# Two empty steps in the preparation of a delta-rule chunk, and shorter steps, in a hybrid flow-matching layer

## The chip, the cores and the metric

The kernel runs on one core of one Trainium2 chip. The metric is the device time of one execution in microseconds (us). The version before took 2160.81 us in the median of 3 runs (2158.47 to 2161.46). The engines are named as in the profile: PE is TensorE's matrix multiply and PEld its weight load, DVE is VectorE, ACT is ScalarE, POOL is GpSimd, and SP is SyncE, which only issues transfers here.

## The reference

One layer is applied to 2048 sample tokens and to 128 prompt tokens. Tokens are normalized and modulated, one wide projection gives the columns of three branches, each branch is gated and projected back, the three results are merged by sigmoid gates, and an output projection and a last norm follow.

```python
def mixer(xn, w_in, conv_w, a_log, dt_bias, o_norm_g, sgu_norm_g, w_spatial, b_spatial, w_branch, w_out, s0_f, s0_b, grid):
    proj = jnp.einsum('btd,de->bte', xn, w_in)
    qkv, beta, dec, z_a, u_b, v_b, z_b, x_c, z_c, gates = jnp.split(proj, points, axis=-1)
    qkv = short_conv(qkv, conv_w).astype(jnp.float32)
...
    o, s_f, s_b = delta_bidir(q, k, v, g, beta, s0_f, s0_b)      # branch A
    o_a = rmsnorm(o, o_norm_g) * silu(z_a)
    o_b = chunk_sgu(u_b, v_b, sgu_norm_g, w_spatial, b_spatial) * silu(z_b)
    o_c = fourier_mix(x_c, grid) * silu(z_c)
    pb = jnp.einsum('btnw,nwd->btnd', jnp.stack([o_a, o_b, o_c], axis=2), w_branch)
    merged = jnp.einsum('btnd,btnd->btd', jax.nn.sigmoid(gates), pb)
    return jnp.einsum('btd,de->bte', merged, w_out), s_f, s_b
```

Branch A is a gated delta rule in both directions over chunks of tokens. For each chunk it needs the products of the keys with each other and of the queries with the keys, and the inverse of a unit triangular matrix per head; then a scan over the chunks carries a 128x128 state per head.

## The kernel before

**Stages.** Every product of float32 matrices is made of three float16 products (high by high, high by low, low by high), so almost every value is split into a high half (ACT) and a low half (DVE). TensorE runs through the foreground in this order: the modulated tokens and branch A's gate, the q, k and v projections with their convolutions, branch B's v (the spatial gating, "sg" and "vs" in the profile), B's u and gate in four groups ("vrow"), branch C's Fourier mixing in four groups ("xc", "Y", "X", "yT"), the merge of branches B, C and A, and the output projection.

**The background.** Branch A's delta rule is a generator, `delta()`. It is advanced by `pace`: each foreground unit reports what it costs TensorE with `pace.tick`, and `Pace.steps` (L331 on) takes one step of the generator for each `quota` us so reported. The quota is `QUOTA` (1.6) during the preparation and `SCAN` (1.39) from the scan on. A step is what lies between two `yield`s. What each step issues goes into the instruction streams of all engines beside the foreground's, and a scheduler then orders each engine's stream; the engines execute their streams strictly in that order.

**Preparation of one chunk.** There are 17 chunks of 128 tokens, in five groups of 1, 4, 4, 4 and 4; below they are counted from first to seventeenth in this order. `prep` (L694) has seven steps for a chunk. Step 1 turns the keys (`turned(1)`: four transposes on TensorE, L702, of the tile "kq") and norms them into `tok` (DVE, L719). Step 2 turns the values ("kq" too) and the queries ("qr", L702), and splits the queries (L728, L729). Step 3 turns the normed keys back (L735) into the high and low halves of `T` (ACT L736, DVE L737). Step 4 makes the twelve products of T with itself on TensorE and the first of two scaled matrices on DVE (L751), its diagonal blocks (ACT L753) and its halves (L755, L756); step 5 makes the second. Step 6 stores the diagonal blocks (POOL, L760), makes the products of queries and T, and the first of two scaled results (DVE L766, ACT L768, DVE L769); step 7 makes the second. All these products go to three PSUM banks in rotation (`ps_d`). So the values are turned into the bank that the products of T had, which DVE's L751 must have read, and the queries into the bank that the products of queries and T had, which L766 must have read.

**The base inverses.** For each group, `base_inverse` (L780) inverts the 32x32 diagonal blocks on DVE: it loads them (SP, L789), lets eight steps pass, copies a half (L792), runs 31 pairs of dependent small operations (L799, L800), and splits the result (ACT L806, DVE L807, four times). `delta()` advances the base of one group by one step after each step of `prep` of the next group; its eight waiting steps add no `yield` there, its 19 others add one each. The base of the last group runs beside the scan.

**The scan.** After the last chunk, `scan()` loads the stored pieces and carries the state forward and backward. `finish_delta` takes whatever is left of it at the start of the last column block of the merge of branch C.

Of the kernel before, what the change touches and what calls it, by code (L numbers as in the profile page):

```python
# [28 lines left out]
WB = 512  # L29
EPS = 1e-6  # L30
C_QKV, C_BD, C_ZA, C_U, C_V, C_ZB, C_XC, C_ZC, C_G = 0, 1536, 1552, 2064, 2576, 3088, 3600, 4112, 4624
QUOTA = 1.6
SCAN = 1.39
MT = 0.015
XB = 4
# [76 lines left out]
def hybrid_flow_kernel(ctx: ExitStack, tc: tile.TileContext, x_prompt, x_sample, state_delta, c, c_ctx, ln_g, w_ada,  # L112
# [6 lines left out]
    def nm(s):  # L119
        uid[0] += 1  # L120
        return f"{s}_{uid[0]}"
# [4 lines left out]
    def sb(pl, shape, tag, dt=F32, bufs=None):  # L126
        kw = {} if bufs is None else {"bufs": bufs}
        return pl.tile(list(shape), dt, tag=tag, name=nm(tag), **kw)
# [11 lines left out]
    def bank(pl, shape, tag="b"):  # L140
        if pl is ps_d:
            rot[0] += 1
            pl = ps_d[rot[0] % 3]
        return pl.tile(list(shape), F32, tag=tag, name=nm(tag))
# [18 lines left out]
    def mm3(out, l, r):  # L163

        mm(out, l[0], r[0], True, False)
        mm(out, l[0], r[1], False, False)
        mm(out, l[1], r[0], False, True)
# [511 lines left out]
    def rows(part, t):  # L679
        x = sb(d2, [P, H, P], "kq" if part else "qr", bufs=3 if part else 2)  # L680
        SY.dma_start(x, qkvD[part * 4:part * 4 + 4, :, chunk_off(t):chunk_off(t) + P].rearrange("h p t -> p h t"))
        return x
# [3 lines left out]
    def late(dst, src):  # L686

        if owed:
            SY.dma_start(*owed.pop())
        if dst is not None:  # L690
            owed.append((dst, src))

    def prep(g, ci, t, nxt, held):
# [18 lines left out]
        def more(key, make):  # L712
            if nxt is not None:
                held[key] = make()
# [14 lines left out]
        V.scalar_tensor_tensor(Q16[:, 1, :], qr, qs, Q16[:, 0, :], ALU.mult, ALU.subtract)  # L729
        yield 1  # L730
        G.dma_start(kvD[t], tok)
        T = sb(d2, [P, 2, WB], "T", F16)
        ps = bank(ps_d, [P, WB])
        for h in range(H):
            PE.transpose(ps[:, hs(h)], tok[:, 0, hs(h)], ident)  # L735
        A.activation(T[:, 0, :], ps, AF.Copy, scale=FS)  # L736
        V.scalar_tensor_tensor(T[:, 1, :], ps, FS, T[:, 0, :], ALU.mult, ALU.subtract)  # L737
        more(2, lambda: rows(2, nxt))
        late(qTD[t], Q16)
        yield 1  # L740
        late(kTD[t], T)
        dc = cur["dc"]
        ps = bank(ps_d, [P, WB])
        pair = lambda t_, h: (t_[:, 0, hs(h)], t_[:, 1, hs(h)])
        for h in range(H):
            mm3(ps[:, hs(h)], pair(T, h), pair(T, h))
        nd = sb(d2, [P, 2, H, 32], "nd", bufs=2)
# [14 lines left out]
        for h in range(H):  # L762
            mm3(ps[:, hs(h)], pair(T, h), pair(Q16, h))
        for d in range(2):
# [324 lines left out]
    def delta():  # L1089
        nonlocal dq  # L1090
        seq = [(g, ci, t) for g, ts in enumerate(GROUPS) for ci, t in enumerate(ts)]
        held = {1: rows(1, 16), 2: rows(2, 16), 0: rows(0, 16), "dc": decay_rows(16)}
        yield from bounds()
        base = iter(())
        for i_, (g, ci, t) in enumerate(seq):
            if ci == 0 and g:
                for r_ in base:
                    if r_:
                        yield 1
                base = base_inverse(g - 1)  # L1100
            for n_, _ in enumerate(prep(g, ci, t, seq[i_ + 1][2] if i_ < 16 else None, held)):
                yield 1
                if next(base, 0):
                    yield 1
        late(None, None)
        for r_ in base:
            if r_:
                yield 1
        base = base_inverse(4)
        dl.close()  # L1110
        dq = pool(dl, "dqb", 1, side="right")
        V.tensor_scalar(rq, rq, bnds[:, 2:3], None, ALU.mult)
        V.tensor_scalar(beta, beta, FS, None, ALU.mult)
        for d in range(2):
            V.tensor_tensor(eg[:, d], eg[:, d], rq, ALU.mult)
        pace.quota, pace.fine = SCAN, True
        for i_, _ in enumerate(scan()):
            yield 1
            if i_ % 3 == 0:
                next(base, 0)  # L1120
        dl.close()
        dps.close()

    pace.start(delta(), QUOTA)

# [735 lines left out]
```

## Time and profile before

| | before |
|---|---|
| median of 3 runs, us | 2160.81 (2158.47 to 2161.46) |
| the profiled execution, us | 2162.01 |
| its span, first to last instruction, us | 2160.1 |
| mean granted TensorE clock | 0.994 |
| PE busy, us (share of the span) | 2098.5 (97%) |
| DVE busy, us (share) | 1403.5 (65%) |
| ACT busy, us (share) | 1057.6 (49%) |
| instructions | 43209 |

The profile comes from one execution, which ran 1.2 us above the median of the runs; 1.9 us of its time lie outside its span. In a row of a timeline stand the start, the duration, the engine, the line with its operation and, in brackets, how long the engine had been idle before it and what ended that. In a row of the waits stand the waiting instruction, what it waited for, the sum in us, how many times, and the longest. In a row of a table of stretches stand the stretch in us, the busy time of each engine with its count of instructions, the granted clock, the share of the DMA engines and GB/s. In a row of the groups stand line, engine, operation and shapes, the count, the busy time and the mean of one in ns, and the idle time before them.

### The profile page before, as it was taken

Reading aid. Unit: us, or ns where it says so; the run is one execution under the profiler, and the core shown is the slowest. Engines: PE = TensorE matmul, PEld = TensorE weight load, DVE = VectorE, ACT = ScalarE, POOL = GpSimd, SP = SyncE. Lnnn points to the kernel's source line nnn. Section 1 sums busy time; section 2 is a strip of 40 time slices with the busy share of each in tenths; the row PEclk is TensorE's granted clock in tenths of the full one; section 3 lists DMA queues with packets and bytes.
Section 4 is the critical chain, followed back from the end, with each engine's and each line's share of the span. In section 5 each row is a group of like instructions: output and inputs, shape, how many; then the busy total and the mean of one; then the engine's idle time right before and its main releaser. Section 6 shows DMA issues by size and latency. Waiting matters only on the chain.

```text
span 2160.1 us, 43209 instructions
## 1 busy us (share of the span) xinstructions
PE 2098.5 (97%) x16275; PEld 1208.3 (56%) x16275; DVE 1403.5 (65%) x3241; ACT 1057.6 (49%) x2463; POOL 735.8 (34%) x872
## 2 busy tenths in 40 slices
PE   7999999999999999999999999999999999999898
PEld 3555444455555577788656556555564444444344
DVE  5745855469888697776665546765564546754685
ACT  3644644445556565554654445655553435323452
POOL 1430533232333334233322223354542221224662
PEclk9999999999999999999999999999999999999999
DMA  8434733266776765444565555767665547544554
GB/s 278 145 94 138 265 103 111 92 191 203 249 241 224 215 193 161 126 131 145 191 201 162 158 168 176 240 194 225 183 198 182 178 141 220 175 139 156 195 175 157
DMA packets 321499, 384.54 MB, mean 178 GB/s; under 512 B 40721, under 2 KB 227322, under 8 KB 318858
## 3 DMA queue, kind: packets, MB, share of 16 engines
q1 hardware_dynamic: 305946, 321.33, 48.2%
q0 software_dynamic: 12752, 51.27, 6.6%
q10 hardware_dynamic: 2592, 9.18, 1.1%
q8 instruction: 128, 2.10, 0.4%
q14 instruction: 81, 0.66, 0.1%
HBM read 246.72 MB, written 134.96 MB: 177 GB/s over the span
## 4 chain that ended last, share of the span: by engine, by line
PE 49%; DVE 6%; DMA 5%; ACT 2%; issue 2%; POOL 1%; SPq 0%; POOLq 0%; ACTq 0%; DVEq 0%
PE b L161 49%; DMA wst<-in_w_branch_dram 1%; DMA wst<-in_w_in_dram 1%; DVE xl L1628 1%; DMA st<-br 1%; DMA mt<-mrg 1%; DMA mrg<-mrow 0%; DVE E L800 0%; PE b L1061 0%; DVE XB L799 0%; DVE wlo L225 0%; DMA big<-br 0%; DMA XB<-nd 0%; DVE blo L225 0%; DMA qk<-n 0%
## 5 line engine op out<-in xcount | busy, mean ns | idle before, releaser
L161 PE MATMUL b<-xl,whi 128*128 128x512 f16 (+1 forms) x1920 | 650.3, 347 | 0.0
L161 PE MATMUL b<-xh,whi 128*128 128x512 f16 (+1 forms) x1920 | 649.7, 347 | 0.1
L161 PE MATMUL b<-xh,wlo 128*128 128x512 f16 (+1 forms) x1920 | 649.6, 347 | 0.0
L161 PEld LDWEIGHTS <-whi 128*128 128x128 f16 x3840 | 350.7, 98 | 316.1 <-issue 4.0
L161 PEld LDWEIGHTS <-wlo 128*128 128x128 f16 x1920 | 187.9, 98 | 173.4 <-issue 0.7
L161 PE MATMUL b<-big,bhi 128*128 128x512 f16 (+1 forms) x960 | 249.7, 347 | 2.5 <-DVE big L1374 1.7
L161 PEld LDWEIGHTS <-xl 128*128 128x128 f16 x1488 | 140.1, 99 | 101.2 <-issue 10.2
L1428 POOL TENSOR_TENSOR mrow<-mrow,sg 128x512 f32<-128x512 f32 (+1 forms) x80 | 102.7, 1287 | 269.9 <-DVE sg L1427 207.3
L161 PE MATMUL b<-big,blo 128*128 128x512 f16 (+1 forms) x480 | 163.2, 347 | 0.2 <-DVE blo L225 0.2
L1381 ACT ACTIVATE sg<-b,winv 128x512 f32<-128x512 f32 (+1 forms) x120 | 74.0, 617 | 134.3 <-PE b L161 133.3
L648 POOL TENSOR_TENSOR cy<-cy,raw 128x545 f32<-128x545 f32 (+1 forms) x48 | 75.3, 1595 | 181.2 <-ACT raw L647 181.2
L161 PEld LDWEIGHTS <-xh 128*128 128x128 f16 x1496 | 118.4, 99 | 28.0
L161 PEld LDWEIGHTS <-bhi 128*128 128x128 f16 x960 | 86.8, 98 | 78.4 <-issue 2.1
L211 ACT ACTIVATE wlo<-wst 128x1024 f16<-128x1024 f32 x52 | 55.0, 1058 | 98.2 <-DMA wst<-in_w_in_dram 96.5
L868 POOL COPY T<-ES 32x256 f16<-32x256 f16 x68 | 30.4, 447 | 201.8 <-DMA ES<-ei 198.3
L161 PE MATMUL b<-whi,xh 128*128 128x128 f16 x544 | 95.1, 221 | 0.0
L161 PE MATMUL b<-wlo,xh 128*128 128x128 f16 x544 | 95.1, 221 | 0.0
L161 PE MATMUL b<-whi,xl 128*128 128x128 f16 x544 | 95.0, 221 | 0.0
L1427 DVE SCALAR_TENSOR_TENSOR sg<-b,binv,sg 128x512 f32<-128x512 f32 (+1 forms) x80 | 53.3, 666 | 61.2 <-PE b L161 54.9
L225 DVE SCALAR_TENSOR_TENSOR wlo<-wst,wsc,whi 128x1024 f16<-128x1024 f32 x52 | 71.0, 1370 | 32.6 <-ACT whi L224 31.7
L175 DVE CAST wscb<-wss 128x1 bf16<-128x1 f32 x85 | 12.8, 152 | 118.6 <-ACT wlo L211 74.0
L161 PE MATMUL b<-gq,xl 128*128 128x512 f16 x384 | 88.6, 387 | 0.0
(504 smaller groups left out, 4294.0 us busy)
## 6 DMA issues: line engine op xcount, KB each, us to landing
wst<-in_w_in_dram SPq DMA_DIRECT2D x60, 512.0 KB
qkv<-cy POOLq DMA_DIRECT2D x12, 1089.0 KB, 5.2
st<-br SPq DMA_DIRECT2D x40, 256.0 KB
mrow<-mrg SPq DMA_DIRECT2D x16, 576.0 KB
dc<-dec SPq DMA_DIRECT2D x17, 512.0 KB
kq<-qkv SPq DMA_DIRECT2D x34, 256.0 KB
kv<-tok POOLq DMA_DIRECT2D x17, 512.0 KB, 5.1
n<-n SPq DMA_DIRECT2D x34, 256.0 KB
```

The lines of the kernel that those rows point to most:

```text
L161: return PE.matmul(out, l, r, start=start, stop=stop)
L175: V.tensor_copy(sb16, ss)
L211: A.activation(w.lo, st, AF.Square, accum_out=ss)
L225: V.scalar_tensor_tensor(w.lo, st, s, w.hi, ALU.mult, ALU.subtract)
L648: G.tensor_tensor(y[:, c0:c1], y[:, c0:c1], raw[:, 1 + c0:1 + c1], ALU.mult)
L868: G.tensor_copy(T16[rows(a0, b), :, :, b], ES[0:32, :, 2 * a0 + b, :, wT])
L1381: A.activation(sg, ps, AF.Sigmoid, scale=gw.inv)
L1427: V.scalar_tensor_tensor(sg, ps, binv[:, 1:2], sg, ALU.mult, ALU.mult)
L1428: G.tensor_tensor(mr, mr, sg, ALU.add)
L1628: V.scalar_tensor_tensor(lo, src, s, hi, ALU.mult, ALU.subtract)
```

## The change

`prep` gets two more `yield`s that issue nothing between them: one ahead of the transposes that make T, one ahead of T's products. A chunk then takes nine steps where it took seven: T's transposes stand in step 4 and T's products in step 6. `QUOTA` goes from 1.6 to 1.4, which shortens every step of the preparation, those of the base inverses in it too. Lines behind the first new `yield` are one higher, and behind the second two higher than before.

```diff
-QUOTA = 1.6
+QUOTA = 1.4
...
         V.scalar_tensor_tensor(Q16[:, 1, :], qr, qs, Q16[:, 0, :], ALU.mult, ALU.subtract)
         yield 1
         G.dma_start(kvD[t], tok)
+        yield 1
         T = sb(d2, [P, 2, WB], "T", F16)
         ps = bank(ps_d, [P, WB])
         for h in range(H):
...
         late(qTD[t], Q16)
         yield 1
         late(kTD[t], T)
+        yield 1
         dc = cur["dc"]
         ps = bank(ps_d, [P, WB])
```

By the code, the preparation has 17 x 7 = 119 steps before and 17 x 9 = 153 after, to which the bounds add 4 and the four base inverses that run in it 4 x 19 = 76. At 1.6 us each that is 199 x 1.6 = 318.4 us of reported foreground work before, and 233 x 1.4 = 326.2 us after.

Two places of VectorE's stream, each before and after. The first is the sixth chunk, the first of the third group: the rows go from the normed keys (tok, L719) to the low half of T (L737, after the change L738) and the first half of the base's copy and pairs (XB and E).

```order
L719 TENSOR_TENSOR tok_5758<-b_5762,ss_769_5759 128x512
L709 TENSOR_SCALAR ss_769_5759<-ss_769_5759 128x4
L1224 SCALAR_TENSOR_TENSOR vrow_5650<-b_5817,winv_4240,vrow_5650 128x512
L792 COPY XB_5775<-XB_5775 64x1024
L799 TENSOR_TENSOR XB_5775<-XB_5775,E_5776 128x31
L800 TENSOR_TENSOR E_5776<-E_5776,XB_5775 128x31
L799 TENSOR_TENSOR XB_5775<-XB_5775,E_5776 128x60
L800 TENSOR_TENSOR E_5776<-E_5776,XB_5775 128x30x2
L799 TENSOR_TENSOR XB_5775<-XB_5775,E_5776 128x87
L737 SCALAR_TENSOR_TENSOR T_5806<-b_5807,T_5806 128x512
```

The same place of VectorE's stream in the changed kernel, where the copy is L794 and the pairs are L801 and L802:

```order
L719 TENSOR_TENSOR tok_5758<-b_5762,ss_769_5759 128x512
L771 SCALAR_TENSOR_TENSOR n_767_5754<-n_766_5752,n_767_5754 128x512
L709 TENSOR_SCALAR ss_769_5759<-ss_769_5759 128x4
L1137 SCALAR_TENSOR_TENSOR sg_5898<-b_5873,winv_4540,sg_5898 128x512
L738 SCALAR_TENSOR_TENSOR T_5834<-b_5835,T_5834 128x512
L794 COPY XB_5775<-XB_5775 64x1024
L801 TENSOR_TENSOR XB_5775<-XB_5775,E_5776 128x31
```

The base's copy, which waits for a load, and its first pairs stood ahead of T's low half and now stand behind it.

The second place is the sixteenth chunk in the changed kernel, in the first group of the Fourier stage: VectorE's stream from the low half of T (L738) to the scaled matrix (n, L753), which empties the bank of T's products. XB and E are the base's last pairs, L809 its conversions, sg, X and yT are branch C's.

```order
L738 SCALAR_TENSOR_TENSOR T_9149<-b_9150,T_9149 128x512
L801 TENSOR_TENSOR XB_8053<-XB_8053,E_8054 128x87
L802 TENSOR_TENSOR E_8054<-E_8054,XB_8053 128x3x29
L801 TENSOR_TENSOR XB_8053<-XB_8053,E_8054 128x60
L802 TENSOR_TENSOR E_8054<-E_8054,XB_8053 128x2x30
L801 TENSOR_TENSOR XB_8053<-XB_8053,E_8054 128x31
L802 TENSOR_TENSOR E_8054<-E_8054,XB_8053 128x31
L809 SCALAR_TENSOR_TENSOR XB_8053<-E_8054,XB_8053 128x16x32 x4
L1137 SCALAR_TENSOR_TENSOR sg_9185<-b_9160,zc_8267,sg_9185 128x512
L1297 TENSOR_TENSOR X_1126_8259<-b_9197,X_1126_8259 128x4x65
L1297 TENSOR_TENSOR X_1126_8259<-b_9197,X_1126_8259 128x4x63
L1316 TENSOR_TENSOR yT_8265<-b_9216,us_9241 128x8x32
```

Behind these stand one more row of yT and the eight of L753. Before the change too the conversions stood between this chunk's T and its scaled matrix, but TensorE, which needs that bank free for the seventeenth chunk's values, had 61 products of 512 columns and 63 smaller ones between this chunk's products of T and those transposes. Now it has 33 small products, and both times the four transposes of the keys. On TensorE the rows at the keys' transposes are now:

```order
L161 MATMUL b_9378<-q_1202_9085,T_9149 128x128
L702 MATMUL b_9455<-cst_87,kq_8996 128x128 x4
L161 LDWEIGHTS Y_1129_8266
L161 MATMUL b_9280<-cf_1427,Y_1129_8266 128x128
L161 LDWEIGHTS Y_1129_8266
```

The keys' transposes follow the sixteenth chunk's last product of queries and T (q and T) at once, and the values' come 15 small products later. In VectorE's and TensorE's streams the order of the first three chunks is the same before and after.

## The prediction

> **What bounds the kernel now.** I read the page's busy times first, then the waits of TensorE in order of their sum, then its timeline at each wait with VectorE's and ScalarE's beside it, and last the table of stretches for the granted clock.
>
> ```profile
> PE 2098.5 (97%) x16275; PEld 1208.3 (56%) x16275; DVE 1403.5 (65%) x3241; ACT 1057.6 (49%) x2463; POOL 735.8 (34%) x872
> ```
>
> TensorE's stream is 2098.5 us of work in a span of 2160.1 us. The change adds and removes no operation, so this work stays; only the 61.6 us in which TensorE idles can change, and the time that it runs at a lower clock.
>
> ```profile
> PE b L161 <- ACT T L736: 4.8, 3, 2.5
> PE b L161 <- DVE T L737: 3.2, 3, 1.5
> PE b L735 <- DVE tok L719: 2.9, 2, 2.0
> PE b L702 <- issue: 2.6, 2, 2.4
> PE b L161 <- DVE sg L1197: 1.8, 3, 0.9
> PE b L702 <- DVE n L751: 0.6, 1, 0.6
> ```
>
> In the preparation, 450 to 840 us, these are TensorE's waits: 4.8 + 3.2 + 2.9 + 2.6 + 1.8 + 0.6 = 15.9 us. The first two are T's products waiting for T, the third T's transposes waiting for tok, which are the two places that get an empty step. The others are banks that VectorE has not yet read, and branch B's own.
>
> ```profile
> 520.00:560.00 40.00, 39.05 (x249) 23.25 (x248) 39.44 (x116) 21.16 (x65) 13.14 (x19) 1.00 0.71 219
> 720.00:760.00 40.00, 40.00 (x220) 20.70 (x219) 22.47 (x54) 20.87 (x69) 10.99 (x15) 1.00 0.76 222
> 760.00:800.00 40.00, 35.88 (x552) 33.06 (x549) 39.10 (x108) 24.92 (x80) 16.71 (x24) 1.00 0.58 186
> 489.08 0.23 PE L161 MATMUL b<-T 128*128 128x128 f16 x1 [2.49 <-ACT T L736]
> 579.95 0.78 PE L161 MATMUL b<-T 128*128 128x128 f16 x11 [1.47 <-DVE T L737]
> 609.95 0.63 PE L702 MATMUL b<-cst,qr 128*128 128x128 f32 x4 [2.41 <-issue]
> 714.10 0.23 PE L161 MATMUL b<-T 128*128 128x128 f16 x1 [2.12 <-ACT T L736]
> 763.06 0.63 PE L735 MATMUL b<-cst,tok 128*128 128x128 f32 x4 [1.98 <-DVE tok L719]
> 768.54 0.77 PE L161 MATMUL b<-T 128*128 128x128 f16 x11 [1.33 <-DVE T L737]
> L792 DVE COPY XB<-XB 64x1024 f32<-64x1024 f32 x5 | 5.3, 1058 | 15.7 <-DMA XB<-nd 10.5 <-DMA n<-n 2.9 <-DMA qT<-q 2.3
> 710.44 3.12 ACT L806 ACTIVATE XB<-E 128x512 f16<-128x512 f32 x4 [3.91 <-DVE E L800]
> 712.10 2.58 DVE L807 SCALAR_TENSOR_TENSOR XB<-E,XB 128x512 f16<-128x512 f32 x3 [0.31 <-ACT XB L806]
> ```
>
> The reader is to see a pattern. VectorE is full (39.44 and 39.10 of 40 us) where a base inverse runs beside a chunk, and half idle (22.47) where none does. The waits come at two moments of a base. Its first copy waits for its load, 15.7 us in 5 copies, and whatever stands behind it on VectorE is late: T at 489 and 580, tok and T at 763 and 768. And its conversions take ScalarE for 3.12 us ahead of T's high half: T at 714.
>
> **The change part by part.** *Total length.* The preparation grows from 318.4 to 326.2 us of reported work, so the scan starts and ends some 8 us later, up to the 16 that the streams show. That costs nothing as long as foreground is left to cover it:
>
> ```profile
> L1061 PE MATMUL b<-cst,o x68: 272/273/330, 1292.2 to 1653.6; 128*128 128x128 f32 x68
> 1684.41 0.17 PE L161 MATMUL b<-bscb,ones 128*128 128x1 bf16 x1
> ```
>
> The scan's last transposes start at 1653.6 us, and the block before which the rest is drained shows its scale's product at 1684.41: 31 us are left, and 16 are used. I take 0, with ends of 0 and, if it were drained, a few us.
>
> *Waits that stay.* The streams of the first three chunks are unchanged, so the 2.49 us at 489 and branch B's 1.8 us stay: 0.
>
> *Waits that lose their cause.* At the sixth chunk the base's copy moves behind T's low half: the 1.47 us go. The tok of that chunk waited 0.96 us (2.9 less 1.98), and L735 now comes a step later: gone. At the twelfth, the conversions move behind T: the 2.12 us go, and what the two other waits leave of the low half's 3.2 us, 0.4. At the fourteenth and fifteenth the tok has a step more: 1.98, 1.33, the values' 0.6 (L702 on L751) and the 0.2 left of the high half's 4.8 go. The queries' 2.6 us on a bank I let go too: the chunks ahead of them start without a wait. Sum: 1.47 + 0.96 + 2.12 + 0.4 + 1.98 + 1.33 + 0.6 + 0.2 + 2.6 = 11.7 us. The ends are 0 (all return elsewhere) and 11.7.
>
> ```profile
> 608.00:612.00 4.00, 2.05 (x14) 0.88 0.89 262
> 612.00:616.00 4.00, 4.00 (x15) 0.69 1.06 352
> 488.00:492.00 4.00, 2.92 (x36) 1.00 0.17 66
> ```
>
> After the 2.41 us wait at 610 the granted clock was 0.88 and 0.69 for 4 us each, which cost 0.12 x 4 + 0.31 x 4 = 1.7 us more; after the 2.49 us at 489 it stayed 1.00. So with the wait at 610 goes 1.7 us: 13.4 us in all.
>
> [...]
>
> *Waits that come.* (a) At the fifth chunk the conversions of the first base now stand right ahead of T's low half, as at the twelfth before, which cost 2.12 + 0.4 = 2.5 us there; but the tok is a step earlier. I take 1.0, between 0 and 2.5. (b) At the fourteenth chunk the copy, with a wait of 15.7 / 5 = 3.1 us in the mean, now stands two operations ahead of T's low half. As the tok and T's neighbours (0.7 us each) now come ahead of it, it waits 3.1 - 1.4 = 1.7 us; I take half of that, 0.8, between 0 and the 2.5 us that a copy ahead of T cost at 489. (c) The base's operations come at 2.8 us a step and chunk step where it was 3.2, so VectorE is denser while a base lasts; the banks of the eighth, ninth and twelfth chunks are close: 1.0, between 0 and 3. (d) The sixteenth chunk. Between its T and the release of the bank of T's products VectorE has six small pairs, four conversions, a gate, two pieces of X, two of yT and the eight of L751:
>
> ```profile
> 802.86 0.18 DVE L800 TENSOR_TENSOR E<-E,XB 128x31 f32<-128x31 f32 x1
> 714.60 0.67 DVE L737 SCALAR_TENSOR_TENSOR T<-b,T 128x512 f16<-128x512 f32 x1
> 771.54 2.15 DVE L751 SCALAR_TENSOR_TENSOR n<-b,beta,dc 128x128 f32<-128x128 f32 x8
> L1135 DVE SCALAR_TENSOR_TENSOR sg<-b,zc,sg 128x512 f32<-128x512 f32 x4 | 3.0, 746 | 2.9 <-ACT sg L1133 2.9
> L1295 DVE TENSOR_TENSOR X<-b,X 128x260 f16<-128x260 f32 x4 | 1.7, 425 | 0.0
> L1315 DVE TENSOR_TENSOR yT<-b,us 128x256 f32<-128x256 f32 x3 | 1.8, 597 | 0.0
> 802.96 0.68 DVE L737 SCALAR_TENSOR_TENSOR T<-b,T 128x512 f16<-128x512 f32 x1
> 805.86 0.78 PE L161 MATMUL b<-T 128*128 128x128 f16 x11
> ```
>
> From ScalarE's start on the conversions at 710.44 to the T behind them at 714.60 are 4.2 us. With six pairs of some 0.2 us each (the last one 0.18), 0.7 for the gate, 0.8 for X, 1.1 for yT and 2.15 this is 1.2 + 4.2 + 0.7 + 0.8 + 1.1 + 2.15 = 10.1 us, or 9.7 with the rows' overlap. TensorE has 45 products and 8 transposes in that time; 11 products take 0.78 us with their drain, some 0.06 each, and four transposes 0.6: 3.3 to 3.9 us. T itself was 2.2 us early at this chunk before (done at 803.64, used at 805.86). So TensorE waits 9.7 - 3.3 - 2.2 = 4.2 us, between 0 and 6.4, and as that is longer than 2.41 us I add 1.7 us of clock: 5.9. Sum of what comes: 1.0 + 0.8 + 1.0 + 5.9 = 8.7 us.
>
> *The entry into the scan.*
>
> ```profile
> 831.29 0.72 PE L161 MATMUL b<-q,T 128*128 128x128 f16 x10
> 851.82 0.63 ACT L913 ACTIVATE v<-sv 128x512 f16<-128x512 f32 x1 [7.70 <-DMA sv<-kv]
> 852.99 0.23 PE L161 MATMUL b<-cf,xc 128*128 128x128 f16 x1 [2.40 <-ACT xc L1277]
> 855.18 1.25 PE L161 MATMUL b<-cf,xc 128*128 128x128 f16 x10 [1.88 <-DVE xc L1278]
> 856.00:860.00 4.00, 4.00 (x40) 0.50 0.31 87
> 860.00:864.00 4.00, 4.00 (x73) 0.97 0.09 33
> ```
>
> ScalarE waits for the scan's first load until 851.82, 20 us after the last products of queries and T (832), with the first split of a Fourier group behind it. TensorE loses 2.40 + 1.88 = 4.3 us and, at half the clock for 4 us, 2 us more. In the changed stream the wait stands behind the third split, and TensorE needs the fourth after 240 products: 240 x 4 / 73 = 13 us. So it would stand still for 20 - 13 = 7 us where it was 4.3: 2.7 more. VectorE's last work on the chunk starts before these products now (L751, 2.15 us, stood behind them), which brings the load forward by part of that: I take 1.5 us, between -6.3 (no wait at all) and 2.7. For the scan's other waits, which meet other foreground, I take 0, with 2.5 us to both sides.
>
> **Sum.** 2162.0 (the profiled execution) - 13.4 + 8.7 + 1.5 = 2158.8 us. That execution ran 1.2 us above the median, so against the median of 2160.8 I predict 2157.6: 0.15% less, which is about what a measurement of this kernel can tell from no change (0.2%, 4.3 us).
>
> **The rivals.** *Faster by over 0.2%* (the waits go and little comes): if (d) stays below the 2.41 us that cost clock, the price of what comes falls from 8.7 to 2.8 + 2.4 = 5.2 us, and without the entry's 1.5 the time is 2157.6 - 3.5 - 1.5 = 2152.6. For it: VectorE has empty time in a chunk after a base (22.47 of 40), and a base's 28 steps now fill a little over three chunks of nine steps where they filled four of seven. Against it: the counted 9.7 us at the sixteenth chunk. *Slower* (VectorE becomes the bound at the last base in the preparation): that base starts later in its chunk, so 61 of its 62 small operations fall in the next two chunks, beside the Fourier stage, where VectorE was at 39.10 of 40 us already. Then the waits of 1.98, 1.33, 0.6 and 0.2 us there return (4.1), and the wait at the bank costs its 6.4 + 2 where I took 5.9 (2.5): 2157.6 + 4.1 + 2.5 + 1.2 (the entry's upper end) = 2165.4. It decides from the point where TensorE's waits between the fourteenth chunk's T and the seventeenth chunk's values pass 12 us in all, twice what I count. *The change does nothing that it says*: the first three chunks keep their order, and if the scheduler's order matters and not the steps, the waits only move. That is 2158 to 2163, and it is counted with no change.
>
> **How the numbers follow.** My forecast of 2157.6 with what only moves waits, 2156.5 to 2165.1, gets 0.42, the faster case 0.40, the slower 0.18; these are the chances of same, faster and slower. The forecast's own range is 2154 to 2162. For 8 in 10 the range goes from 2149 (the faster case, with 3.5 us of the entry's or the scan's waits gone) to 2166 (the slower case).
>
> **What would show it.** Right: no wait of T's products on T from the sixth chunk on, above all none at the twelfth; the wait at 489 unchanged; a wait of 2 to 6 us of L702 on VectorE, or of X, near 820 us, with a lower clock behind it. Wrong: the sum of T's and tok's waits above 6 us; no wait at the seventeenth chunk's values; waits on xc at the scan's entry above 9 us or below 3; the scan's last transposes behind 1684 us.

## The result, and the profile after

| | before | after |
|---|---|---|
| median, us | 2159.64 (4 runs, 2157.12 to 2161.46) | 2173.68 (4 runs, 2170.63 to 2175.13) |
| profiled execution, us | 2162.01 | 2174.29 |
| its span, us | 2160.1 | 2172.2 |

The changed kernel is slower: the ratio is 1.0053, with a 95% interval of 1.0038 to 1.0069 (the quotient of the two medians above, 1.0065, lies inside it). The prediction (2157.6 us, 2149 to 2166) is missed by 16 us and on the wrong side. Line numbers of the changed kernel are one or two higher than before.

First the page's busy row of the changed kernel, then some of its waits of TensorE, the largest first (us in total, times, longest):

```profile
PE 2103.0 (97%) x16275; PEld 1212.9 (56%) x16275; DVE 1404.5 (65%) x3241; ACT 1061.5 (49%) x2463; POOL 733.4 (34%) x872
```

```profile
PE b L161 <- ACT v L915: 6.1, 2, 4.2
PE b L161 <- DVE X L1298: 5.6, 4, 1.9
...
PE b L161 <- ACT xc L1279: 3.8, 1, 3.8
PE b L161 <- DVE T L738: 3.7, 1, 3.7
...
PE b L702 <- DVE n L753: 2.6, 2, 2.2
```

The instructions are the same; the idle time is 2172.2 - 2103.0 = 69.2 us where it was 61.6. Of the waits of T, tok and the queries that the change aimed at, two of T (3.70 and 1.07 us) and 0.27 us of tok are left, and new names stand near the head of the list: v, X and xc, all between 820 and 980 us but one wait on v of 1.92 us at 1091. TensorE's timeline at its long waits between 450 and 1000 us, and the table of stretches of 4 us for the granted clock (the column behind the count):

```profile
487.47 0.23 PE L161 MATMUL b<-T 128*128 128x128 f16 x1 [1.07 <-ACT T L737]
678.15 0.66 PE L702 MATMUL b<-cst,kq 128*128 128x128 f32 x4 [2.22 <-DVE n L753]
765.90 1.33 PE L161 MATMUL b<-T 128*128 128x128 f16 x11 [3.70 <-DVE T L738]
825.20 0.33 PE L161 MATMUL b<-cf,X 128*128 128x128 f16 x3 [1.61 <-DVE X L1298]
868.18 0.40 PE L161 MATMUL b<-cf,xc 128*128 128x128 f16 x2 [3.80 <-ACT xc L1279]
897.36 0.33 PE L161 MATMUL b<-cf,X 128*128 128x128 f16 x3 [1.54 <-DVE X L1298]
912.94 0.22 PE L161 MATMUL b<-u,kn 128*128 128x128 f16 x1 [0.87 <-ACT u L915]
925.67 0.27 PE L161 MATMUL b<-v,R 128*128 128x128 f16 x1 [4.15 <-ACT v L915]
```

```profile
676.00:680.00 4.00, 1.85 (x10) 0.94 0.78 230
680.00:684.00 4.00, 4.00 (x14) 0.63 0.83 264
764.00:768.00 4.00, 2.10 (x21) 0.61 0.39 141
768.00:772.00 4.00, 4.00 (x43) 0.54 0.19 52
828.00:832.00 4.00, 3.89 (x24) 0.78 0.68 227
868.00:872.00 4.00, 3.81 (x11) 0.50 0.96 238
924.00:928.00 4.00, 2.33 (x23) 0.66 0.64 181
```

Five of these waits are followed by a lower clock, where before the change two places were (610 and 853 us). To compare kernels I add up, for a stretch, the waits that TensorE's timeline puts in brackets, and for the clock (1 - granted clock) x busy time over all stretches of 4 us:

| us | 0 to 450 | 450 to 840 | 840 to 1000 | 1000 to 1700 | 1700 to the end | sum |
|---|---|---|---|---|---|---|
| before: waits + clock | 16.3 + 2.3 | 16.5 + 1.5 | 5.5 + 2.5 | 8.7 + 0.0 | 5.5 + 3.3 | 62.0 |
| after: waits + clock | 16.0 + 3.8 | 13.2 + 5.6 | 12.8 + 4.1 | 11.5 + 0.0 | 6.7 + 1.6 | 75.4 |
| difference | +1.3 | +0.8 | +8.9 | +2.8 | -0.4 | +13.4 |

The two profiled executions differ by 12.3 us, so this account is nearly whole. The preparation (450 to 840) gained nothing; the entry into the scan lost 8.9 us and the scan's later steps 2.8.

**The preparation.** VectorE's timeline of the changed kernel, with ScalarE's row of the fourteenth chunk's T:

```profile
674.85 1.06 DVE L794 COPY XB<-XB 64x1024 f32<-64x1024 f32 x1 [5.32 <-DMA XB<-nd]
675.94 2.16 DVE L753 SCALAR_TENSOR_TENSOR n<-b,beta,dc 128x128 f32<-128x128 f32 x8
...
759.31 0.62 ACT L737 ACTIVATE T<-b 128x512 f16<-128x512 f32 x1
...
763.65 1.03 DVE L794 COPY XB<-XB 64x1024 f32<-64x1024 f32 x1 [4.46 <-DMA XB<-nd]
...
765.16 0.68 DVE L738 SCALAR_TENSOR_TENSOR T<-b,T 128x512 f16<-128x512 f32 x1
```

The two long waits of the preparation, at 678 and 765, both stand behind a base's first copy that waits for its load with VectorE's queue behind it, as the waits of T and tok did before. The five copies wait as they did, 16.2 us where it was 15.7; what stands behind them has changed. In these rows VectorE did nothing while the copy waited, with work ready behind it: T's high half was done at 759.93 us, and its low half, which stands behind the copy, started only at 765.16, 1.5 us after a copy that had waited 4.46 us.

**The entry.** The timeline of the changed kernel at the scan's first u and second v, on VectorE (DVE), ScalarE (ACT) and SyncE's queue (SPq):

```profile
907.21 0.68 DVE L1009 TENSOR_TENSOR sv<-b,beta 128x512 f32<-128x512 f32 x1
...
907.32 3.14 ACT L808 ACTIVATE XB<-E 128x512 f16<-128x512 f32 x4 [0.56 <-DVE E L802]
...
907.98 3.85 DVE L809 SCALAR_TENSOR_TENSOR XB<-E,XB 128x512 f16<-128x512 f32 x4
...
910.13 4.94 SPq L812 DMA_DIRECT2D ei<-XB  x4
...
912.25 0.63 ACT L915 ACTIVATE u<-sv 128x512 f16<-128x512 f32 x1
...
915.17 2.96 SPq L956 DMA_DIRECT2D sv<-kv  x1
...
923.83 1.12 DVE L987 SCALAR_TENSOR_TENSOR sv<-b,neg,sv 128x128 f32<-128x128 f32 x4 [8.67 <-DMA sv<-kv]
...
924.99 0.63 ACT L915 ACTIVATE v<-sv 128x512 f16<-128x512 f32 x1 [5.98 <-DVE sv L987]
```

and ScalarE before the change:

```profile
885.86 3.14 ACT L806 ACTIVATE XB<-E 128x512 f16<-128x512 f32 x4 [3.11 <-DVE E L800]
898.32 0.64 ACT L913 ACTIVATE u<-sv 128x512 f16<-128x512 f32 x1
```

The last base runs beside the first steps of the scan. Before, its conversions were done 9 us ahead of the scan's first u. Now they start at 907.32, when u's source has just been written (907.21), and u is split only at 912.25. Its source has one buffer, which is free only then, and the base's own writes stand ahead in SyncE's queue; so the next load (915.17) and the next v (924.99) are late too: 0.87 + 4.15 us for TensorE, and a lower clock behind it. The rest of what this stretch lost is 4.0 us of waits on X (897, 962 and 978 us), where the kernel before had none; no run takes these away without others coming.

### The profile page after: what moved, and what is told of

Read it like the earlier page. It is cut to its first block, busy times and chain, and to the rows that moved or that the text cites. A ratio compares the mean times of both kernels' runs of the same rounds, so it can differ in the third digit from the quotient of the medians.

```text
span 2172.2 us, 43242 instructions
## 1 busy us (share of the span) xinstructions
PE 2103.0 (97%) x16275; PEld 1212.9 (56%) x16275; DVE 1404.5 (65%) x3241; ACT 1061.5 (49%) x2463; POOL 733.4 (34%) x872
## 5 line engine op out<-in xcount | busy, mean ns | idle before, releaser
L175 DVE CAST wscb<-wss 128x1 bf16<-128x1 f32 x85 | 12.9, 153 | 122.4 <-ACT wlo L211 74.4
```

Source lines behind the costliest of these rows:

```text
L175: V.tensor_copy(sb16, ss)
```

## The experiments

Each ratio is to the kernel before, run on the same chip beside it, with its 95% interval. In the table "waits" are TensorE's bracketed waits of the profiled execution, each counted once, in the stretch in which it ends.

| kernel | median, us | ratio | interval | 450 to 840 | 840 to 1000 | 1000 to 1700 | all waits | clock |
|---|---|---|---|---|---|---|---|---|
| before | | 1 | | 16.5 | 5.5 | 8.7 | 52.5 | 9.5 |
| the change | 2173.68 | 1.0053 | 1.0038 to 1.0069 | 13.2 | 12.8 | 11.5 | 60.2 | 15.2 |
| conv_after_u | 2165.85 | 1.0037 | 1.0022 to 1.0052 | 12.3 | 11.1 | 10.7 | 54.1 | 15.2 |
| base_after_u | 2173.51 | 1.0061 | 1.0046 to 1.0076 | 13.8 | 13.9 | 10.2 | 59.3 | 10.6 |
| steps_ontime | 2173.21 | 1.0059 | 1.0046 to 1.0072 | 19.4 | 8.9 | 8.6 | 61.0 | 13.1 |
| quota_only | 2165.65 | 1.0029 | 1.0014 to 1.0044 | 14.9 | 7.9 | 11.6 | 55.7 | 7.8 |
| delay10 | 2177.54 | 1.0076 | 1.0061 to 1.0091 | 16.0 | 5.7 | 19.1 | 65.3 | 11.4 |
| delay5 | 2173.24 | 1.0060 | 1.0045 to 1.0076 | 16.4 | 5.6 | 17.2 | 58.9 | 15.6 |
| delay1 | 2174.69 | 1.0065 | 1.0048 to 1.0083 | 12.9 | 6.3 | 15.2 | 56.3 | 14.6 |
| head13 | 2162.20 | 1.0009 | 0.9998 to 1.0021 | 14.4 | 6.7 | 9.8 | 51.2 | 12.9 |
| early8_after | 2171.74 | 1.0052 | 1.0040 to 1.0064 | 13.9 | 11.0 | 13.2 | 61.2 | 13.8 |
| early8_vlate_before | 2170.83 | 1.0046 | 1.0029 to 1.0062 | 15.5 | 8.5 | 10.2 | 57.7 | 8.2 |
| first_yield | 2171.07 | 1.0044 | 1.0030 to 1.0057 | 16.1 | 8.6 | 13.8 | 61.7 | 10.9 |
| second_yield | 2169.25 | 1.0041 | 1.0029 to 1.0054 | 12.4 | 8.6 | 13.3 | 56.2 | 11.7 |
| after_q138 | 2184.05 | 1.0122 | 1.0101 to 1.0143 | 16.9 | 11.2 | 16.7 | 68.1 | 11.1 |
| copyT_after | 2172.27 | 1.0047 | 1.0029 to 1.0065 | 16.9 | 10.9 | 11.5 | 60.3 | 14.6 |
| copyT_vlate_after | 2173.02 | 1.0051 | 1.0037 to 1.0066 | 15.6 | 11.7 | 13.1 | 63.0 | 11.9 |
| vlate_before | 2158.00 | 0.9987 | 0.9975 to 0.9999 | 13.7 | 6.5 | 9.0 | 49.5 | 9.3 |
| copyT_vlate_before | 2151.13 | 0.9964 | 0.9950 to 0.9978 | 11.1 | 5.5 | 8.3 | 47.5 | 9.5 |
| copyT_before | 2152.54 | 0.9963 | 0.9949 to 0.9977 | 9.9 | 7.4 | 4.8 | 42.9 | 7.6 |

### Is it the last base at the scan's entry?

Two kernels move the last base against the scan's first u and leave all else of the changed kernel; `tc.issue_after` adds an edge that puts an instruction behind another on its engine. Two more take the change apart: its steps without its length, its length without its steps.

conv_after_u (`first_u` holds the two instructions of the scan's first split of u):

```diff
+                with ExitStack() as st_:
+                    if first_u:
+                        st_.enter_context(tc.issue_after(first_u[0][0]))
+                        st_.enter_context(tc.issue_after(first_u[0][1]))
                     A.activation(both[:, js, 0, w, :], src[:, js], AF.Copy, scale=FS)
                     V.scalar_tensor_tensor(both[:, js, 1, w, :], ...)
```

> The changed kernel with one edge of order: the last base's four conversions stand behind the split of the scan's first u on ScalarE and VectorE, where they stood ahead of it. Theory A (the late base delays u, and through u's buffer the next v): the waits on u (0.87 us) and v (4.15 us) near 912 and 925 us go, and with them the 1.7 us of lower clock behind the second: 2173.7 - 6.7 = 2167.0, within 2. Rival B (the nine steps cost the time in the preparation, the entry's waits would come anyway from the late load): v's wait stays between 3 and 5 us and the time at 2173.7, within 2.

base_after_u (the copy, with all that hangs on it, behind the same split):

```diff
+            if first_u:
+                st_.enter_context(tc.issue_after(first_u[0][1]))
             V.tensor_copy(b3(X[64:P, :]), ...)
...
-            if i_ % 3 == 0:
+            if i_ > 12 and i_ % 3 == 0:
                 next(base, 0)
```

> The changed kernel with the whole last base behind the first u on VectorE, so that it does not run beside the first Fourier stage X. Theory A: the waits on u and v and the first wait on X (1.54 us near 897) go: 2173.7 - 0.87 - 4.15 - 1.7 - 1.54 = 2165.4, within 2. Rival B: 2173.7 within 2. Rival C (VectorE is full anyway, what goes here comes back at the second X near 962 to 978, which waited 0.59 and 1.85): X's waits there rise above 5 us and the time is 2168 to 2172.

steps_ontime:

```diff
-QUOTA = 1.4
+QUOTA = 1.3665
```

> The changed kernel's nine steps with a quota of 1.3665 instead of 1.4, so that the preparation reports 233 x 1.3665 = 318.4 us as before the change and the scan starts some 8 us earlier. The order shows the last base's conversions behind the first u here, but still behind the X pieces of the first Fourier stage. Theory A: no wait on v above 1 us near the entry, so about 6.7 us less: 2167.0 within 3. Rival B (nine steps as such): 2173.7 within 2. Rival D (any lateness of the scan): all the entry's waits go back to 5.5 us and the time to 2162 within 2.

quota_only (in the kernel before):

```diff
-QUOTA = 1.6
+QUOTA = 1.639
```

> The kernel before, seven steps, with a quota of 1.639 instead of 1.6: 199 x 1.639 = 326.2 us, the changed kernel's length without its steps. The order shows the last base's conversions right ahead of the first u, as in the changed kernel. Theory A: the waits on u and v come without any new step, 5.0 us and 1.7 of clock: 2159.6 + 6.7 = 2166.3, within 3. Rival B (nine steps cost the time): 2159.6 within 2.

TensorE's timeline of conv_after_u, of base_after_u and of steps_ontime, at the long waits:

```profile
931.23 0.22 PE L161 MATMUL b<-S,sk 128*128 128x128 f16 x1 [2.74 <-ACT S L921]
931.95 0.77 PE L161 MATMUL b<-S,sk 128*128 128x128 f16 x11 [0.51 <-DVE S L922]
```

```profile
912.13 0.47 PE L161 MATMUL b<-R,Q 128*128 128x64 f16 x10 [3.63 <-DVE Q L908]
955.35 0.27 PE L161 MATMUL b<-S,sk 128*128 128x128 f16 x1 [4.26 <-ACT S L920]
```

```profile
872.81 0.19 PE L161 MATMUL b<-ES,N 128*128 128x32 f16 x1 [6.11 <-POOL T L870]
```

In conv_after_u the waits on u and v are gone, as theory A said; that the conversions made them is shown. But a new wait of 3.25 us on S stands 6 us later, and though the median (2165.85) is what theory A gave, the gain cannot be told from none: 1.0037 against the change's 1.0053, with intervals that overlap. With the whole base moved, Q and S wait 7.9 us instead, and nothing is gained. steps_ontime loses the waits on u and v too, has the scan's later waits back at 8.6, and is as slow as the change: its preparation waits 19.4 us, and 6.11 us come at 872. quota_only came out at the time that theory A gave, but not in its way: no wait on u or v near 912 us is in its profile. Theory A names a true wait and does not explain the time.

### Is it the scan's lateness?

delay10, and delay5 and delay1 with 5 and 1 in the place of 10 (in the kernel before):

```diff
+        for _ in range(10):
+            yield 1
         pace.quota, pace.fine = SCAN, True
```

> The kernel before with ten empty steps of 1.6 us each between the last chunk of the preparation and the scan: the scan's products come some 16 us later, the preparation and the last base keep their order. Theory A' (it is the last base's place against the Fourier stage and the preparation's own waits that cost, not the scan's lateness): 2160.7 within 2.5, TensorE's waits between 840 and 1000 us between 4 and 8 us. Rival D (a scan that starts later meets other foreground at each of its steps, or pushes the end): 2166 to 2173, with its waits between 1000 and 1700 us above 11 or the end's above 7.

> The kernel before with five empty steps of 1.6 us between the preparation and the scan, half of the ten that cost 16 us: the scan comes as late as in the changed kernel (8 us), and nothing else moves. Theory F (the scan's lateness has a price of its own, in its later steps): TensorE's waits between 1000 and 1700 us at 10.5 to 14 where 8.7 were, time 2160.7 + 3 to 8, so 2166 within 3. Rival (only the sixteen us were too much, because a load or the end was met): 2160.7 within 2 and waits of 8 to 9.5 there.

> The kernel before with one empty step of 1.6 us between the preparation and the scan. (1) lateness has a price that grows with it: a fifth of what five steps cost, 2160.7 + 2.6 = 2163.3, within 2. (2) any shift loses the fit: 2166 to 2173, with TensorE's waits between 1000 and 1700 us above 10.5 where 8.7 were.

head13 (in the kernel before), and early8_after (8 for 14 in the changed kernel):

```diff
-        for _ in range(14):
+        for _ in range(13):
             yield 1
```

> The kernel before with 13 empty steps of 1.39 us at the head of the scan instead of 14: the scan 1.4 us earlier. (1): 2160.7 or 1 to 2 us less, 2159.5 within 2. (2): 2166 to 2173, as with a later scan.

> The changed kernel with 8 empty steps of 1.39 us at the head of the scan instead of 14: the nine steps of the preparation and its quota stay, but the scan's products come some 8 us earlier, as early as before the change; by the order the last base's conversions then stand behind the first u. Theory F: the waits on u and v and the clock behind them (6.7 us) go, and the waits between 1000 and 1700 us return from 11.5 to 8.5 to 9.5: 2173.7 - 6.7 - 2.5 = 2164.5, within 3. Rival B (the nine steps themselves cost the time): 2173 within 2, with the gain at the entry given back elsewhere.

The table of stretches (busy time of TensorE) from 1000 to 1700 us, of the kernel before and of delay1, and TensorE's and ScalarE's timelines of delay1:

```profile
1000.00:1700.00 700.00, 691.18 (x6124) 1.00 0.61 186
```

```profile
1000.00:1700.00 700.00, 684.82 (x6036) 0.99 0.61 183
```

```profile
1389.33 0.77 PE L1061 MATMUL b<-cst,o 128*128 128x128 f32 x2 [2.41 <-ACT o L1057]
```

```profile
1387.74 0.72 ACT L1375 ACTIVATE big<-st,bsc 128x512 f16<-128x512 f32 x1 [3.12 <-DMA st<-br]
1388.88 0.69 ACT L1057 ACTIVATE o<-o,oss 128x128 f32<-128x128 f32 x2
```

A single empty step of 1.6 us, with the order of TensorE, VectorE and ScalarE as it was up to 864 us, makes the kernel 0.65% slower, as much as five and nearly as much as ten. The loss is in the scan's later steps: 6.4 us more idle there, and 4.1 us of clock (this execution ran 5.6 us below the median of delay1, so it shows about half of what the step cost). At 1389 us TensorE waits for o, and ScalarE had waited 3.12 us for a load of the foreground with o behind it: the copy's pattern with other names. So lateness costs, but not in proportion to it, and all three delays cost more than the expectations gave. It is not a fixed price either: quota_only, which spreads the same 8 us over the preparation, costs 0.29% where delay5 costs 0.60%. Nor does taking it away help: with the scan 8 us earlier the changed kernel stays at 1.0052, though its waits on u and v fell from 5.0 to 1.8 us. Only head13, 1.4 us earlier, stays where the kernel before was, between what the two theories gave.

### Other shifts

first_yield and second_yield have one of the two new steps each, and a quota that keeps the preparation's length (the diff is that of the second):

```diff
-QUOTA = 1.6
+QUOTA = 1.474
...
         late(kTD[t], T)
+        yield 1
```

> The kernel before with the first empty step alone (ahead of T's transposes), eight steps, quota 1.474, so 216 x 1.474 = 318.4 us as before. By (2), any shift of the steps against the foreground loses the fit: 2166 to 2175. If only the second step did harm: 2160.7 within 2.

> The kernel before with the second empty step alone (ahead of T's products), eight steps, quota 1.474 so that the preparation reports 216 x 1.474 = 318.4 us as before. Theory A'' (the prediction's: a step ahead of the products takes their wait on T): no wait of T's products above 1 us from the sixth chunk on, and with the scan on time 2157 to 2161. Rival B (any denser steps make waits elsewhere, as the nine steps on time did, 2173): 2166 to 2173.

after_q138 is the changed kernel with another quota:

```diff
-QUOTA = 1.4
+QUOTA = 1.38
```

> The changed kernel with a quota of 1.38 instead of 1.4: the same nine steps, 233 x 1.38 = 321.5 us, 3 us longer than before the change. (1): between the 2173.2 of the quota on time and the 2173.7 of the change, so no change: 2173.5 within 2. (2): another draw from the same distribution, anywhere in 2165 to 2178; below 2163 would say that nine steps cost nothing by themselves.

early8_vlate_before is vlate_before (below) with `range(8)` at the scan's head:

> The kernel before with the first v and S split behind Q (2158.0 before) and 8 empty steps at the head of the scan instead of 14, so that the scan comes 8 us earlier than before the change. If lateness alone sets the scan's waits they fall below 8.7 and the time to 2153 within 3. Rival (before stands at the best place of its kind, any shift to either side costs): 2160 to 2168.

Each step alone costs nearly what both cost at the old length (0.44 and 0.41%, where steps_ontime has 0.59), and in second_yield the waits of T's products are gone as meant (0.57 us is the longest from the sixth to the sixteenth chunk). after_q138 lost 1.2%, more than either expectation allowed: 16.9 us of waits in the preparation and 16.7 in the scan's later steps. Of eleven shifts to either side besides the change itself (quota_only, steps_ontime, the three delays, head13, early8_after, early8_vlate_before, the two steps, after_q138) ten are slower by 0.3 to 1.2% and one is the same; none is faster.

### Taking the wait away without a shift

copyT puts each base's first copy behind T's low half (`last_t` holds the instruction that split T last):

```diff
-        V.scalar_tensor_tensor(T[:, 1, :], ps, FS, T[:, 0, :], ALU.mult, ALU.subtract)
+        last_t[:] = [V.scalar_tensor_tensor(T[:, 1, :], ps, FS, T[:, 0, :], ALU.mult, ALU.subtract).ins]
...
+        with tc.issue_after(last_t[0]):
             V.tensor_copy(b3(X[64:P, :]), ...)
```

vlate puts the scan's first split of v, and that of S, behind the first split of Q:

```diff
+                if i_ == 0:
+                    st_.enter_context(tc.issue_after(first_q[0][0]))
+                    st_.enter_context(tc.issue_after(first_q[0][1]))
                 split(v16, v_)
```

> The changed kernel with one edge of order: each base's first copy stands behind the low half of T of the same chunk on VectorE. Theory A: the wait on T at the fourteenth chunk (3.70 us in the changed kernel's profile, 1.6 and 1.9 in the two kernels above that share its order there) and the 3.4 us of lower clock behind it go: 3 to 7 us less than 2173.7, so 2168.7 within 2.5. Rival E (the base then ends later and costs the same at X or at the seventeenth chunk's bank): waits between 760 and 840 us stay at 4.5 to 6.5 and the time at 2173, within 2.

> The changed kernel with both edges: first copies behind T, the first v and S behind Q. The order then shows the last base's conversions behind the first u as well. Theory A: the wait on xc (3.80 us) with its clock (3.4), on T (3.70, or 1.6 to 1.9) with its clock (up to 3.4), on u and v (5.0) with 1.7 go: between 2173.7 - 14 = 2160 and 2173.7 - 20 = 2154. Rival B (these waits are only the visible end of a chain that is late anyway, as in the run in which the whole base was put behind u and nothing was gained): above 2168.

> The kernel before with the split of the scan's first v (and S) behind the first small split of the scan (Q) on ScalarE and VectorE, so that the splits xc of the Fourier stage no longer stand behind the wait for the load of v. If the entry's wait is what the prediction said, the 2.40 + 1.88 us at 853 and 855 go and 3.4 us of lower clock with them: 2160.7 - 7.7 = 2153.0, within 3. Rival: the splits are then late for another reason, or Q waits: 2160.7 within 2.

> The kernel before with the bases' first copies behind T's low half and the scan's first v and S split behind Q (the latter alone: 2158.0, 0.13% less than before): no step is shifted. (2) the fit stays: 2158 less the waits of tok and T at the fifteenth chunk (1.98 + 1.33) if the copy made them, so 2154.5 to 2158. Rival: the copies' place reorders enough that it costs as the other shifts did, 2166 to 2173.

> The kernel before with one edge: each base's first copy behind T's low half on VectorE, no step shifted. If the copies ahead of T are what T waits for, the waits at 489, 580, 763 and 768 us (2.49, 1.47, 1.98, 1.33) go or shrink below 1 us, and the time is what both edges gave plus what the other one gave alone: 2151.1 + 2.7 = 2153.8, within 2.5. Rival (the gain needs both edges, or was a fit of the order as a whole): 2158 to 2163.

In the changed kernel neither helps: with copyT the 3.70 us of T go, and 3.89 us come at X, whose pieces VectorE now takes behind the last of the base's conversions and the whole scaled matrix (at 823.84 us, where it was 821.93); v still waits. With both edges v no longer does, and 4.40 us at 875 and 2.10 us on u come.

```profile
827.57 2.74 PE L161 MATMUL b<-cf,X 128*128 128x128 f16 x24 [3.89 <-DVE X L1301]
925.47 0.22 PE L161 MATMUL b<-v,R 128*128 128x128 f16 x1 [2.80 <-ACT v L918]
```

In the kernel before, vlate takes the wait on xc and its clock, and some smaller waits come; 0.13% are left. copyT gives 0.37%. The waits of copyT_before's TensorE on T from 450 to 840 us, and VectorE's timeline:

```profile
PE b L161 <- DVE T L739: 2.8, 3, 1.7
...
PE b L161 <- ACT T L738: 0.6, 1, 0.6
```

```profile
485.10 1.07 DVE L795 COPY XB<-XB 64x1024 f32<-64x1024 f32 x1
...
663.21 1.06 DVE L795 COPY XB<-XB 64x1024 f32<-64x1024 f32 x1
...
753.93 1.07 DVE L795 COPY XB<-XB 64x1024 f32<-64x1024 f32 x1
```

Of the waits of 2.49, 1.47, 1.98 and 1.33 us none is left above 0.4, and three of the five copies no longer wait at all; 1.7 us at 819, which are new, make up half of the waits on T. This is what the change set out to do with steps, and it holds in the kernel before: both versions of it with this edge beat both kernels, and from 450 to 840 us waits and clock fell from 16.5 + 1.5 to 9.9 + 0.0 us, about the 7 to 8 us of the gain. The waits from 1000 to 1700 us fell from 8.7 to 4.8 us as well, but not by the edge: TensorE's order there is that of before, the profiled execution was the fastest of its five, and with both edges the waits are 8.3 and the time is the same. So a few us in that column are what executions of one order differ by.

## Why the prediction was wrong

**Waits that stay.** The 2.49 us at 489 are 1.07 now, and branch B's 1.8 are 2.1. Six kernels above that keep the order of before there (the delays, head13 and the two with vlate and without copyT) show 1.00 to 1.22: the profiled execution of before was high at this place. The base's first copy just ahead waited 2.45 us for its load there and 0.97 to 1.18 in the six, and each time T's wait is the copy's to within 0.05 us. A single wait of one execution was taken for a fixed number.

**Waits that go** (13.4 us with the clock). Right: each of them is gone, the one at the twelfth chunk too, and the clock at 610 (1.7 us as counted there, 1.5 by busy time).

**Waits that come in the preparation** (8.7 us). (a) Fifth chunk, 1.0: nothing came. (b) The copy ahead of T at the fourteenth chunk, 0.8 with a bound of 2.5: 3.70 us and 0.39 x 2.10 + 0.46 x 4 = 2.7 of clock. The mean of five copies (3.1) was put in and half of what was left of it taken; this copy waited 4.46 us, and 4.57 in the kernel before. (c) VectorE denser, 1.0: 2.22 us at the tenth chunk, which was not on the list, with 1.6 of clock, and 1.37 at two more banks; again a copy, of 5.32 us. (d) 5.9: 0.50 + 1.61 + 0.35 us and 1.4 of clock, 3.8. What was to be -4.7 became +0.8: the copies still stop VectorE, and the waits changed their names. The first error is to count a wait as gone when its cause only gets another neighbour.

VectorE's timeline of the kernel before, at that copy:

```profile
755.75 1.06 DVE L792 COPY XB<-XB 64x1024 f32<-64x1024 f32 x1 [4.57 <-DMA XB<-nd]
```

**The entry** (1.5 us). The wait on xc did not grow, 3.80 us where it was 4.28 in two. But nothing was put in for the last base, whose conversions were 9 us ahead of u and fell on it (0.87 + 4.15 us and the clock), nor for X (4.0 us). The stretch lost 8.9 us: this is the term that missed most, by 7.4 us.

**The scan's other waits** (0, within 2.5) **and the total length** (0). This is the step that fails by itself. The length does not run out, though the scan's last transposes came 26 us later and not 16: they start at 1680.0 us, 17 us ahead of the block's product (1697 us now). But to start the scan at another point changes what stands ahead of what all through it: TensorE's order differs from before up to some 1660 us in each of the shifted kernels. Here these later steps lost 2.8 us; in delay5, which only shifts the scan, they lost 13.1 (waits and clock), and the whole cost is 0.60%. So a later scan was put at nothing because foreground was left to cover it, and that was the wrong test.

```profile
L1063 PE MATMUL b<-cst,o x68: 270/273/332, 1313.3 to 1680.0; 128*128 128x128 f32 x68
```

Added up, the prediction had -4.7 + 1.5 + 0 = -3.2 us and the account has +13.4: 5.5 of the 16.6 us between them lie in the preparation, 7.4 at the entry, 2.8 in the scan's later steps and 0.9 outside.

**The slower rival** had VectorE become the bound at the last base in the preparation, at 2165. The sign is right and part of the place: that base gave 3.70 us. It was the next one, in the scan, that cost most.

Of the signs of being wrong that the prediction named none came: T's and tok's waits sum to 5.0 us, 0.35 us are left at the seventeenth chunk's values, xc waits 3.80 us, and the last transposes start at 1680.0 us. It looked for its error where it had priced something, and the loss came where it had put nothing.

What is shown: the change takes the old waits of T and tok away; new ones of the same make come; a later scan alone, by as little as 1.6 us, costs as much as the change. The place where the scan starts does not set the time: early8_after and second_yield start it about where the kernel before does (first u at 897.5 and 896.2 us, where it was 898.3) and have 13.2 and 13.3 us of waits from 1000 to 1700, where that has 8.7. What the traces show beside it is the order of TensorE's instructions. From 893 us on it is that of before in three kernels only, vlate_before, copyT_before and copyT_vlate_before, and these three are the only ones that are faster than before. head13, whose order is another, is the same; every other order is slower by 0.29 to 1.22%. In conv_after_u, base_after_u, copyT_after and copyT_vlate_after it is that of the changed kernel from 990 us on, and these four stay at 1.0037 to 1.0061 whatever was taken away ahead of it. So the time goes with the order of the scan against the foreground; that this order is the cause is argued from these groups and was not tested by itself, and why the order of before fits so well stays open.

## What to carry to other kernels

Where engines take their work in order, look for the instruction that waits for a load at the head of a queue, and put what is urgent ahead of it by an edge of order: that gave 0.37% in the kernel before and nothing in the changed one, while new steps gave the wait another victim. A background stream that is merged with a foreground is a fit: a shift of 1.6 us in 2160 cost 0.65%, and ten of eleven shifts cost something, so a forecast for such a shift of this kernel starts from a loss and not from zero, with a range of a per cent. Before one wait of one profiled execution goes into a sum, see whether it is there in a second one.

## What the runs showed of the hardware

The granted clock fell behind waits of some 2.2 us (0.94 and 0.63 behind the 2.22 us at 678) and not behind every longer one (1.00 behind the 2.49 us at 489 before the change). In the two profiles, before and after, each stretch is at 1.00 or at 0.50 if the cuts are put where the clock changes. Behind the first 60 us of a profile its falls lie whole multiples of 3.413 us apart: in the kernel before they come at 611.05 and at 853.40 us, 71 times that length, and in the changed one at 679.54 and 764.88, 25 times. Four stretches of that length in the kernel before, TensorE alone:

```profile
484.76:488.17 3.41, 1.84 (x9) 1.00 0.67 222
488.17:491.58 3.41, 2.50 (x32) 1.00 0.20 77
607.64:611.05 3.41, 1.10 (x12) 1.00 0.85 236
611.05:614.46 3.41, 3.41 (x10) 0.50 1.03 357
```

The wait at 610 leaves TensorE idle for 3.41 - 1.10 = 2.31 us of one stretch, and the next one runs at 0.50, which costs up to 1.7 us; the wait at 489 lies in two, with 1.57 and 0.91 us idle, and the clock stayed at 1.00. In the two profiles, without the first 60 us and the last 10, a stretch at 0.50 followed one at 1.00 ten times. In the ten ahead of these TensorE was idle for 1.96 to 3.41 us (least at 822.90 us of the changed kernel); where 1.00 followed 1.00 it was idle for 1.82 us at most (at 761.24 us of the kernel before). The length of a wait by itself does not tell: in the changed kernel the 1.61 us on X at 825 were followed by 0.50, the 1.92 us on v at 1091 by 1.00. Of the 13.4 us in the account the lower clock is 15.2 - 9.5 = 5.7: it was nearly half of the loss. The same kernel also scatters more than a single wait can tell: the kernel before ran between 2153.49 and 2168.18 us in the 23 runs beside delay1, and its wait on T at 489 us was 2.49 us in one execution and near 1.1 in six kernels with the same order there.
